# High and low parts of the left operands: two arrays each, or one array with the parts in turn

## The chip, the core and the metric

The kernel runs on one core of a Trainium2 chip. A time is the device time of one execution in microseconds (us). The profile is that of one execution; its span runs from the first to the last instruction that the profile holds. Less is better.

## The reference

One layer of a decoder, for 256 positions and a width of 2048, all in float32. Cut to what matters here:

```python
x = x + 0.5 * swiglu(rms_norm(x, ffn1_norm), ffn1_w_gate, ffn1_w_up, ffn1_w_down)   # width 5632
h = rms_norm(x, mix_norm)
proj = h @ w_in                                   # 10256 columns
aq, ak, av, bq, bk, bv, br, bz, ga, gb = split(proj)
o_a = dilated_attention(rope(rms_norm(aq)), rope(rms_norm(ak)), av)   # 8 heads of 128
log_a = log_sigmoid(bz @ b_gate_w2 + b_gate_bias) / 16                # rank 16
o_b = rms_norm(gated_linear_attention(bq, bk, bv, log_a)) * silu(br)  # 4 heads
y = sigmoid(ga) * (o_a @ w_a_up) + sigmoid(gb) * (o_b @ w_b_up)
x = x + y @ w_out
x = x + 0.5 * swiglu(rms_norm(x, ffn2_norm), ffn2_w_gate, ffn2_w_up, ffn2_w_down)
```

## The kernel before

**Products in three parts.** Nearly all the work is matrix products with large weights. TensorE multiplies operands of the type float32r, which keeps fewer bits than float32. So each operand is held as a high part (the value rounded to float32r) and a low part (the rest), and a product is the sum of three: high x high, high x low and low x high. `split` makes the parts: ScalarE copies the value into the high part, VectorE subtracts that from the value and writes the low part. `split_scaled` does the same with a factor.

**The two sides of a matmul.** The left operand (`lhsT`, the activations, transposed so that the contraction lies on the 128 partitions) is loaded into the array; it is the stationary side, 128 columns wide. The right operand (`rhs`, the weights of the layer, 512 columns) streams through it; it is the moving side. In this text a load is the loading of a stationary operand, which the profile shows as LDWEIGHTS on an engine of its own, PEld. Results are summed in PSUM in two tiles of 128 rows and 512 columns (`acc`, one for each half of the 256 positions, the index t).

**The loop.** All big products are cut into jobs (a block of 512 columns of a weight matrix) and those into steps of two slices of 128 of the contraction. Step i loads 512 KB of weights (`dma_to`), splits them (`split_to`, three steps ahead, into tiles `wh` and `wl`) and issues 12 matmuls (`multiply`, line 150): two slices, two halves of the positions, three products. There are 752 such steps. Other work, such as activations, transposes, the attention and the gated linear attention, is put between the steps by hand-written step numbers and by a list of tasks with costs.

**The left operands.** They are `xh` and `xl` (the normed x, transposed; 16 slices of 256 positions), `fhh` and `fhl` (the inner activations of the first FFN, 44 slices; `shh` and `shl` for the second), `ah` and `al` (outputs of attention, 8 slices) and `bh` and `bl` (outputs of the gated linear attention, 8 slices). In each array the positions of a slice lie next to each other, 4 bytes apart. A load takes 128 of them:

```python
a_hi, a_lo = job.lhs(k, t)
lhsT, rhs = ((a_hi, hi), (a_hi, lo), (a_lo, hi))[j]
nc.tensor.matmul(job.acc[t], lhsT, rhs[:, kk, :], ...)
```

`x_transposed`, `to_lhs`, `y_lhs`, `b_lhs`, the attention's `values` and, for the first norm, `split_xt` write these arrays. One product uses `xh` and `xl` as the moving side: `low_rank` (line 427), 32 matmuls with 32 stationary columns each, for the gate's code z.

**Other names in the rows.** `gram` (line 565), `o` (lines 581 to 583) and `s` (line 730) are plain float32 products of the two attentions, in which the profile shows two passes for each product. Line 550 multiplies `e_tiles` by q or k, in place, at eight levels: at level l it takes runs of 2^l elements and leaves as many out, so at level 0 every second element, on both inputs and the output.

Of the kernel before, what the change touches and what calls it, by code (L numbers as in the profile page):

```python
# [9 lines left out]
F32 = mybir.dt.float32  # L10
F32R = mybir.dt.float32r
# [7 lines left out]
P = 128  # L19
D_MODEL = 2048  # L20
SEQ = 256
D_FF = 5632
NT = SEQ // P
NC = 512
KM = D_MODEL // P
NM = D_MODEL // NC
NF = D_FF // NC
KF = D_FF // P
# [8 lines left out]
BH = 4  # L37
# [20 lines left out]
LINE = 128  # L58
# [11 lines left out]
def hybrid_block(ctx, tc, a):  # L70
    nc = tc.nc
    ctx.enter_context(tc.manual_schedule())
    const = ctx.enter_context(tc.tile_pool(name="const", bufs=1))
# [4 lines left out]
    def side(name):  # L78
        return pside.tile([P, NC], F32, tag="side", name=name)

    x = const.tile([P, NT, D_MODEL], F32, name="x")
    xh = const.tile([P, KM, SEQ], F32R, name="xh")
    xl = const.tile([P, KM, SEQ], F32R, name="xl")


    subs = []
# [6 lines left out]
    def at(step, fn, *args):  # L93
        events.setdefault(step, []).append((fn, args))
# [83 lines left out]
    def finish(flag):  # L178

        while not flag():  # L180
            ready = [t for t in tasks if is_ready(t)]
            assert ready
            run_stage(ready[0])

    def add_task(gen, *needs, delay=2):
        tasks.append({"gen": gen, "needs": needs, "next": now[0] + delay})
# [4 lines left out]
    def row(src, n):  # L191

        return bass.AP(tensor=src.tensor, offset=src.offset, ap=[[0, P], [1, n]])
# [57 lines left out]
    def split(hi, lo, src):  # L251
        nc.scalar.copy(hi, src)  # L252
        nc.vector.tensor_tensor(lo, src, hi.bitcast(F32), op=ALU.subtract)  # L253
# [23 lines left out]
    class FFN:  # L277
# [14 lines left out]
        def open(self):  # L292
            self.stack = ExitStack()
            self.pool = self.stack.enter_context(tc.tile_pool(name=f"{self.name}h", bufs=1))
            self.hh = self.pool.tile([P, KF, SEQ], F32R, name=f"{self.name}hh")
            self.hl = self.pool.tile([P, KF, SEQ], F32R, name=f"{self.name}hl")

        def lhs_h(self, k, t):
            return self.hh[:, k, t * P:(t + 1) * P], self.hl[:, k, t * P:(t + 1) * P]
# [58 lines left out]
    class Mixer:  # L358
# [36 lines left out]
        def open(self, i):  # L395
            self.stack = ExitStack()
            self.pool = self.stack.enter_context(tc.tile_pool(name="mix", bufs=1))
            self.stats = self.t([P, LINE], "stats")
            self.sum_mask = self.t([P, 12, P], "sums", dt=F32R)
            self.wz = self.t([P, KM, 4 * 2 * RANK], "ob", dt=F32R, name="wz_parts")[:, :, :2 * RANK]  # L400
            w = self.t([P, KM, RANK], "temp", 3, name="wz")
            nc.sync.dma_start(w, a["w_z"])
            at(i + 6, split, self.wz[:, :, :RANK], self.wz[:, :, RANK:], w)
            self.w2 = self.t([2 * RANK, NC], "pt", 2, name="w2")
            self.gate_bias = self.t([P, NC], "pt", 2, name="gate_bias")
            for j in range(2):
                nc.sync.dma_start(self.w2[j * RANK:(j + 1) * RANK], a["b_gate_w2"])
            nc.sync.dma_start(self.gate_bias, row(a["b_gate_bias"], NC))

            def load_mask(name, out):  # L410
                m = self.temp(f"c_{name}")
                nc.sync.dma_start(m, a[f"c_{name[:-1]}"][:, 4 * int(name[-1]):][:, :4, :].rearrange("p l t -> p (l t)"))
                out = out.rearrange("p l t -> p (l t)")
                at(now[0] + 3, nc.scalar.copy if out.dtype == F32R else nc.vector.tensor_copy, out, m)

            for j in range(3):
                at(i + 4 + j, load_mask, f"sums{j}", self.sum_mask[:, 4 * j:4 * j + 4, :])
            for j in range(2):
                at(i + 8 + j, load_mask, f"pick{j}", small["pick"][:, 4 * j:4 * j + 4, :])
            at(i + 9, self.low_rank)  # L420
# [32 lines left out]

        def decays(self):

            self.lag = [self.t([P, NT, NC], f"sA{j}", dt=F32R, name=f"lag{j}") for j in range(2)]
            for t in range(NT):
                p = side(f"gate{t}")
                nc.tensor.matmul(p, self.z[:, t * P:(t + 1) * P], self.w2, start=True, stop=True)
                g, e = self.temp(f"gate{t}"), self.temp(f"lse{t}")  # L460
                nc.vector.scalar_tensor_tensor(g, p, norm_mix.r[:, t:t + 1], self.gate_bias,
                                               op0=ALU.mult, op1=ALU.add)
                yield 0.6, 1
                nc.scalar.activation(e, g, AF.Abs)
                nc.scalar.activation(e, e, AF.Exp, scale=-1.0)
                nc.scalar.activation(e, e, AF.Ln, bias=1.0)
                yield 0.0, 1
                nc.vector.scalar_tensor_tensor(e, g, 0.0, e, op0=ALU.min, op1=ALU.subtract)
                yield 0.6, 1
                split(self.lag[0][:, t, :], self.lag[1][:, t, :], e)  # L470
                yield 0.6, 0
            self.flags.add("lag")

        def take_b(self, what, acc):
            r = self.rows(f"{what}_rows")
            for t in range(NT):
                self.scaled(r[:, t, :], acc, t)
            if what == "bk":
                self.bT = self.t([P, 2, BH, SEQ], "bh", name="bT")
            add_task(self.b_transposed(what, r))  # L480

        def b_transposed(self, what, r):
# [121 lines left out]
        def take_br(self, n, acc, t):  # L604
            finish(self.o_done)
            if n == 0 and t == 0:
                self.bh = self.t([P, 8, SEQ], "bh", dt=F32R)
                self.bl = self.t([P, 8, SEQ], "bl", dt=F32R)
            ns = slice(n * NC, (n + 1) * NC)
            e = self.temp(f"br{n}_{t}")  # L610
            nc.scalar.activation(e, acc[t], AF.Tanh, scale=norm_mix.half[:, t:t + 1])
            nc.vector.scalar_tensor_tensor(e, e, 1.0, acc[t], op0=ALU.add, op1=ALU.mult)
            o = self.ob[:, t, ns]
            nc.vector.scalar_tensor_tensor(o, e, norm_mix.half[:, t:t + 1], o,
                                           op0=ALU.mult, op1=ALU.mult)
            if t == NT - 1:
                add_task(self.b_lhs(n))
            return 1.2
# [89 lines left out]
        def attention(self, g):  # L708
            if g == 0:
                finish(self.flag("lag_used"))  # L710
                self.ah = self.t([P, 8, SEQ], "sA0", dt=F32R, name="ah")
                self.al = self.t([P, 8, SEQ], "sA1", dt=F32R, name="al")
            qT, kT, v, ast = self.aT[g][:, 0], self.aT[g][:, 1], self.av[g], self.ast_of[g]
            units = [(0, 0, 4), (1, 0, 2), (1, 2, 2)]
            pts = {}
# [320 lines left out]
```

## Time and profile before

| | us |
|---|---|
| median of 2 runs | 2146.95 (2145.76 to 2148.15) |
| profiled execution | 2146.12 |
| its span | 2144.3 |
| TensorE matmul busy | 2137.9 (100%) |
| TensorE loads busy | 1771.7 (83%) |
| VectorE busy | 1146.1 (53%) |
| ScalarE busy | 946.7 (44%) |

Matmuls are pipelined: a busy interval of TensorE is no proof that it works at its best pace, and the recorded durations of neighbours overlap. The distance from one start to the next is the pace. The ends of matmuls are modelled in the profile.

### The profile page before, as it was taken

How to read it: one execution, taken by the hardware profiler on the slowest of the kernel's cores; microseconds unless marked ns; L12 is line 12 of the kernel's file. 1: busy time of each engine (PE TensorE's matmuls, PEld its weight loads, DVE VectorE, ACT ScalarE, POOL GpSimd, SP SyncE). 2: the span in 40 equal slices, each digit the busy share in tenths (PEclk: the TensorE clock that was granted, in tenths of full speed). 3: DMA queues.
4: the chain of work that ended last, by engine and by line, in shares of the span. 5: the costliest groups of instructions: out<-in, count | busy, mean ns of one | idle time of the engine just before them, and what ended most of it. 6: DMA issues, size and time to landing. Idle time of an engine off the chain costs nothing.

```text
span 2144.3 us, 24974 instructions
## 1 busy us (share of the span) xinstructions
PE 2137.9 (100%) x9684; PEld 1771.7 (83%) x9684; DVE 1146.1 (53%) x1308; ACT 946.7 (44%) x1099; POOL 15.8 (1%) x15
## 2 busy tenths in 40 slices
PE   9999999999999999999999999999999999999999
PEld 7888888888888888888888888888888888888887
DVE  6655555554554456766644466565555555554443
ACT  6444444444444464454444444454444444443332
POOL 0000000000000000000000000000000000000000
PEclk9999999999999999999999999999999999999999
DMA  8666666665565664455566655656666666666663
GB/s 303 205 189 188 192 190 187 190 193 188 191 191 188 190 197 138 149 170 173 170 193 195 194 188 186 188 185 189 191 187 190 189 193 188 188 191 202 205 204 121
DMA packets 114519, 404.53 MB, mean 189 GB/s; under 512 B 13376, under 2 KB 14912, under 8 KB 114400
## 3 DMA queue, kind: packets, MB, share of 16 engines
q1 hardware_dynamic: 114400, 402.93, 60.2%
q8 instruction: 76, 1.25, 0.2%
q14 instruction: 43, 0.35, 0.0%
HBM read 400.79 MB, written 2.10 MB: 188 GB/s over the span
## 4 chain that ended last, share of the span: by engine, by line
PE 99%; DMA 0%; SPq 0%; ACT 0%; DVE 0%; issue 0%; DVEq 0%
PE acc_sg L150 11%; PE acc_fd L150 11%; PE acc_sd L150 11%; PE acc_su L150 11%; PE acc_fu L150 11%; PE acc_fg L150 11%; PE acc_o L150 4%; PE acc_ga L150 4%; PE acc_gb L150 4%; PE acc_aq L150 2%; PE acc_ak L150 2%; PE acc_bv L150 2%; PE acc_br L150 2%; PE acc_av L150 2%; PE acc_ua L150 2%; PE acc_ub L150 2%
## 5 line engine op out<-in xcount | busy, mean ns | idle before, releaser
L253 DVE TENSOR_TENSOR wl_sd<-w_sd,wh_sd 128x1024 fp32r<-128x1024 f32 x88 | 107.8, 1225 | 126.3 <-ACT wh_sd L252 126.3
L253 DVE TENSOR_TENSOR wl_fd<-w_fd,wh_fd 128x1024 fp32r<-128x1024 f32 x88 | 107.8, 1225 | 120.5 <-ACT wh_fd L252 120.2
L253 DVE TENSOR_TENSOR wl_su<-w_su,wh_su 128x1024 fp32r<-128x1024 f32 x88 | 107.8, 1225 | 118.4 <-ACT wh_su L252 118.4
L253 DVE TENSOR_TENSOR wl_fu<-w_fu,wh_fu 128x1024 fp32r<-128x1024 f32 x88 | 107.7, 1225 | 116.7 <-ACT wh_fu L252 113.2
L253 DVE TENSOR_TENSOR wl_sg<-w_sg,wh_sg 128x1024 fp32r<-128x1024 f32 x88 | 107.8, 1225 | 107.8 <-ACT wh_sg L252 107.8
L253 DVE TENSOR_TENSOR wl_fg<-w_fg,wh_fg 128x1024 fp32r<-128x1024 f32 (+1 forms) x90 | 108.1, 1201 | 97.7 <-ACT wh_fg L252 97.7
L252 ACT CAST wh_sd<-w_sd 128x1024 fp32r<-128x1024 f32 x88 | 92.8, 1055 | 146.5 <-PE acc_sd L150 139.8
L252 ACT CAST wh_sg<-w_sg 128x1024 fp32r<-128x1024 f32 x88 | 92.7, 1053 | 134.7 <-PE acc_su L150 66.6
L252 ACT CAST wh_su<-w_su 128x1024 fp32r<-128x1024 f32 x88 | 92.8, 1055 | 133.7 <-PE acc_sg L150 73.2
L252 ACT CAST wh_fg<-w_fg 128x1024 fp32r<-128x1024 f32 (+1 forms) x90 | 93.0, 1034 | 130.4 <-PE acc_fg L150 65.9
L252 ACT CAST wh_fd<-w_fd 128x1024 fp32r<-128x1024 f32 x88 | 92.7, 1053 | 129.5 <-PE acc_fd L150 119.7
L252 ACT CAST wh_fu<-w_fu 128x1024 fp32r<-128x1024 f32 x88 | 92.7, 1055 | 126.7 <-PE acc_fg L150 71.1
L150 PE MATMUL acc_fg<-wh_fg,xh 128*128 128x512 f32 x352 | 138.6, 395 | 0.7 <-DVE xh L873 0.7
L150 PE MATMUL acc_fg<-wl_fg,xh 128*128 128x512 f32 x352 | 137.7, 392 | 0.3 <-DVE wl_fg L253 0.3
L150 PE MATMUL acc_sg<-wh_sg,xh 128*128 128x512 f32 x352 | 137.9, 392 | 0.0
L150 PE MATMUL acc_fd<-wh_fd,fhh 128*128 128x512 f32 x352 | 137.3, 390 | 0.0
L150 PE MATMUL acc_fg<-wh_fg,xl 128*128 128x512 f32 x352 | 137.3, 391 | 0.0
L150 PE MATMUL acc_sg<-wh_sg,xl 128*128 128x512 f32 x352 | 137.1, 389 | 0.0
L150 PE MATMUL acc_sd<-wh_sd,shh 128*128 128x512 f32 x352 | 137.0, 389 | 0.0
L150 PE MATMUL acc_sg<-wl_sg,xh 128*128 128x512 f32 x352 | 137.0, 389 | 0.0
L150 PE MATMUL acc_fd<-wh_fd,fhl 128*128 128x512 f32 x352 | 137.0, 389 | 0.0
L150 PE MATMUL acc_fd<-wl_fd,fhh 128*128 128x512 f32 x352 | 137.0, 389 | 0.0
(306 smaller groups left out, 4985.0 us busy)
## 6 DMA issues: line engine op xcount, KB each, us to landing
w_fu<-in_ffn_w_up SPq DMA_DIRECT2D x88, 512.0 KB, 3.6
w_fd<-in_ffn_w_down SPq DMA_DIRECT2D x88, 512.0 KB, 3.5
w_sg<-in_ffn_w_gate SPq DMA_DIRECT2D x88, 512.0 KB, 3.6
w_su<-in_ffn_w_up SPq DMA_DIRECT2D x88, 512.0 KB, 3.6
w_sd<-in_ffn_w_down SPq DMA_DIRECT2D x88, 512.0 KB, 4.3
w_fg<-in_ffn_w_gate SPq DMA_DIRECT2D x86, 512.0 KB, 3.6
w_ga<-in_w_in SPq DMA_DIRECT2D x32, 512.0 KB, 3.6
w_gb<-in_w_in SPq DMA_DIRECT2D x32, 512.0 KB, 3.5
```

Source lines behind the costliest of these rows:

```text
L150: nc.tensor.matmul(job.acc[t], lhsT, rhs[:, kk, :], start=(k == 0 and j == 0), stop=(k == job.kt - 1 and j == 2))
L252: nc.scalar.copy(hi, src)
L253: nc.vector.tensor_tensor(lo, src, hi.bitcast(F32), op=ALU.subtract)
```

## The change

The two arrays of each left operand become one with a last axis of 2, in which element 0 is the high part and element 1 the low part of the same value. `parts_of` gives the two views, in which neighbours are 8 bytes apart. All functions that write or read left operands work on these views and are otherwise the same. The tile tags follow: `ah` and `al` share the place of `lag` (tag "ap"), `bh` and `bl` that of `bT` (tag "bp"). Two places move: a tile of 8 elements (`to_place`) lies ahead of the FFN's array, which so starts 32 bytes later, and `stats` is 16 elements longer, so that the tiles behind it in the mixer start 64 bytes later, or, behind the joined arrays, elsewhere.

In the built program every engine has the same instructions in the same order as before, with the same waits; tile names, steps and places are what differs.

```diff
     x = const.tile([P, NT, D_MODEL], F32, name="x")
-    xh = const.tile([P, KM, SEQ], F32R, name="xh")
-    xl = const.tile([P, KM, SEQ], F32R, name="xl")
+    def parts_of(t):
+
+        return t[:, :, :, 0], t[:, :, :, 1]
+
+    xh, xl = parts_of(const.tile([P, KM, SEQ, 2], F32R, name="xp"))
...
-            self.hh = self.pool.tile([P, KF, SEQ], F32R, name=f"{self.name}hh")
-            self.hl = self.pool.tile([P, KF, SEQ], F32R, name=f"{self.name}hl")
+            self.pool.tile([P, 8], F32, tag="to_place", name=f"{self.name}to_place")
+            self.hh, self.hl = parts_of(self.pool.tile([P, KF, SEQ, 2], F32R, name=f"{self.name}hp"))
...
-            self.stats = self.t([P, LINE], "stats")
+            self.stats = self.t([P, LINE + 16], "stats")
...
-            self.lag = [self.t([P, NT, NC], f"sA{j}", dt=F32R, name=f"lag{j}") for j in range(2)]
+            lag = self.t([P, 2, NT, NC], "ap", dt=F32R, name="lag")
+            self.lag = [lag[:, j] for j in range(2)]
...
-                self.bT = self.t([P, 2, BH, SEQ], "bh", name="bT")
+                self.bT = self.t([P, 2, BH, SEQ], "bp", name="bT")
...
-                self.bh = self.t([P, 8, SEQ], "bh", dt=F32R)
-                self.bl = self.t([P, 8, SEQ], "bl", dt=F32R)
+                self.bh, self.bl = parts_of(self.t([P, 8, SEQ, 2], "bp", dt=F32R))
...
-                self.ah = self.t([P, 8, SEQ], "sA0", dt=F32R, name="ah")
-                self.al = self.t([P, 8, SEQ], "sA1", dt=F32R, name="al")
+                self.ah, self.al = parts_of(self.t([P, 8, SEQ, 2], "ap", dt=F32R))
```

## Rows read from the trace of the kernel before

**Rows 1.** The page: busy times, granted clock in 40 slices, the chain by engine.

```profile
PE 2137.9 (100%) x9684; PEld 1771.7 (83%) x9684; DVE 1146.1 (53%) x1308; ACT 946.7 (44%) x1099; POOL 15.8 (1%) x15
...
PEclk9999999999999999999999999999999999999999
...
PE 99%; DMA 0%; SPq 0%; ACT 0%; DVE 0%; issue 0%; DVEq 0%
```

**Rows 2.** Waits of PE: us in total, times, longest.

```profile
PE warm L859 <- DVE warm L853: 1.2, 1, 1.2
PE acc_fg L150 <- DVE xh L873: 0.7, 1, 0.7
PE acc_fg L150 <- DVE wl_fg L253: 0.3, 1, 0.3
```

**Rows 3.** Windows, whole span, line 150 alone; the columns are named in the first row.

```profile
core 0: us, PE busy (x) PEld busy (x), PEclk, DMA share, GB/s
0.00:2145.00 2145.00, 2069.28 (x9024) 1690.78 (x9024) 1.00 0.60 189
```

**Rows 4.** Timeline of PE in the steady loop: start, duration, instruction.

```profile
1500.00 0.39 PE L150 MATMUL acc_sg<-wh_sg,xh 128*128 128x512 f32 x1
1500.22 0.39 PE L150 MATMUL acc_sg<-wl_sg,xh 128*128 128x512 f32 x1
...
1504.08 0.39 PE L150 MATMUL acc_sg<-wh_sg,xh 128*128 128x512 f32 x1
```

**Rows 5.** Line 427, the low-rank product: durations, then first and last start.

```profile
L427 PEld LDWEIGHTS z<-xh,wz_parts x16: 107/108/108, 761.6 to 765.3; 128*32 128x32 f32 x16
L427 PE MATMUL z<-xh,wz_parts x16: 280/280/281, 761.9 to 765.4; 128*32 128x256 f32 x16
```

**Rows 6.** Groups by form, a load and a matmul of line 150: busy us, mean ns.

```profile
L150 PEld LDWEIGHTS acc_sg<-wh_sg,xl 128*128 128x128 f32 x352 | 66.1, 188 | 13.8
L150 PE MATMUL acc_sg<-wl_sg,xh 128*128 128x512 f32 x352 | 137.0, 389 | 0.0
```

**Rows 7.** Groups of PEld from 822.59 to 823.9 us, the gram's loads.

```profile
L565 PEld LDWEIGHTS gram<-e_tiles 128*128 128x128 f32 x11 | 1.3, 192 | 0.0
```

**Rows 8.** Timeline of PEld behind the scores' loads.

```profile
1005.28 0.19 PEld L150 LDWEIGHTS acc_br<-wh_br,xh 128*128 128x128 f32 x1
1005.39 0.19 PEld L150 LDWEIGHTS acc_br<-wl_br,xh 128*128 128x128 f32 x1
```

**Rows 9.** Timeline of DVE, line 550: levels 0 to 3, then 4 to 7.

```profile
816.86 1.70 DVE L550 TENSOR_TENSOR e_tiles<-e_tiles,bT 128x128 f32<-128x128 f32 x8
...
819.61 1.70 DVE L550 TENSOR_TENSOR e_tiles<-e_tiles,bT 128x128 f32<-128x128 f32 x8
```

**Rows 10.** Groups of PE from 2140.25 us to the end: the last matmul.

```profile
L150 PE MATMUL acc_sd<-wh_sd,shl 128*128 128x512 f32 x1 | 0.4, 388 | 0.0
```

**Rows 11.** Timeline of PE behind transposes of the attention.

```profile
943.96 0.39 PE L150 MATMUL acc_aq<-wl_aq,xh 128*128 128x512 f32 x1
...
944.42 0.40 PE L150 MATMUL acc_aq<-wh_aq,xh 128*128 128x512 f32 x1
944.66 0.39 PE L150 MATMUL acc_aq<-wl_aq,xh 128*128 128x512 f32 x1
944.88 0.39 PE L150 MATMUL acc_aq<-wh_aq,xl 128*128 128x512 f32 x1
...
946.04 0.39 PE L150 MATMUL acc_aq<-wl_aq,xh 128*128 128x512 f32 x1
```

**Rows 12.** Groups by form, the writers of left operands.

```profile
L253 DVE TENSOR_TENSOR fhl<-fht,fhh 128x512 fp32r<-128x512 f32 x22 | 14.1, 682 | 0.0
...
L249 DVE SCALAR_TENSOR_TENSOR xl<-xt,g_f,xh 128x256 fp32r<-128x256 f32 x16 | 7.3, 480 | 4.3 <-ACT xh L248 4.3
...
L252 ACT CAST fhh<-fht 128x512 fp32r<-128x512 f32 x22 | 11.7, 586 | 0.0
...
L248 ACT ACTIVATE xh<-xt,g_f 128x256 fp32r<-128x256 f32 x16 | 7.1, 471 | 8.0 <-DVE xl L249 8.0
...
L873 DVE TENSOR_SCALAR xh<-x,g_f 128x256 fp32r<-128x256 f32 x4 | 1.4, 351 | 4.4 <-DMA g_f<-in_ffn_norm 3.8 <-DMA x<-in_xT 0.5
```

**Rows 13.** Timeline: the last part of x for the second FFN, and that FFN's first matmul.

```profile
1421.93 0.48 DVE L249 SCALAR_TENSOR_TENSOR xl<-xt,g_f,xh 128x256 fp32r<-128x256 f32 x1 [0.54 <-ACT xh L248]
...
1411.16 0.39 PE L150 MATMUL acc_sg<-wh_sg,xh 128*128 128x512 f32 x1
```

**Rows 14.** Timeline of PE, plain float32 products of the gated linear attention.

```profile
849.67 0.59 PE L581 MATMUL o<-bv_at 128*128 128x256 f32 x2
850.10 0.59 PE L582 MATMUL o<-bv_at 128*128 128x256 f32 x2
850.53 0.59 PE L583 MATMUL o<-bv_at 128*128 128x256 f32 x2
```

## The prediction

> **What bounds the kernel now.** I read the page first: its busy times, its clock line and the chain that ended last [rows 1]. TensorE is busy for 2137.9 us of 2144.3 us, the granted clock stands at 9 tenths or more in all 40 slices, and the chain is 99% TensorE. VectorE is busy for 53% and ScalarE for 44%. The waits of TensorE on others come to 2.2 us, all of them in the start [rows 2]. So the time is the pace of TensorE, and the next view has to say what that pace is made of.
>
> The loop's line L150 issues 9024 matmuls, each with one weight load [rows 3]. The durations in the table of groups (about 389 ns) overlap, so I take the pace from the starts: from 1500.00 to 1504.08 us there are 19 starts, 18 steps in 4.08 us, 226.7 ns each [rows 4]. [...] At one turn (0.417 ns) a column, 512 columns take 213.3 ns, and 13.3 ns of each step are something else. 9024 x 226.7 ns = 2045 us; the other 99 us of the span are small matmuls, transposes, start and tail. The profiled execution took 2146.12 us, 1.8 us more than its span; the median of the two runs shown is 2146.95 us, 0.8 us above it. I sum against 2146.1 and give the result on the median's scale. One nanosecond on the step of the loop is 9.0 us, and 2%, about what a measurement of this kernel can tell from no change, is 42.9 us or 4.8 ns a step.
>
> **The change, part by part.** No instruction is added, removed or moved: every engine's rows stand in the same order with the same waits as before, only under other tile names. So there is no new wait to price. What differs is the step between neighbouring elements (8 bytes in place of 4) of the arrays that hold left operands, and where some tiles lie. This touches four kinds of access.
>
> *1. The weight load.* All 9024 loads of L150 now take every second element of a row. A load of 128 columns is recorded with 188 ns [rows 6], one of 32 columns with 108 ns [rows 5], so a column costs (188 - 108) / 96 = 0.83 ns and 81 ns are a fixed part. How soon loads can follow each other is seen where the matmuls between them are short: eleven loads of the gram lie in 1.3 us, (1300 - 192) / 10 = 111 ns apart [rows 7], and two loads of L150 itself start at 1005.28 and 1005.39 us, 110 ns apart [rows 8]. In the steady loop a load starts as the matmul ahead of it starts, and has 226.7 ns. So 116 ns of each step are free on the load side. The trace shows no load with an 8-byte step. Its bounds: at the same 0.83 ns a column nothing changes; at twice that (one column in two turns) loads follow at 111 + 107 = 218 ns, still under 226.7, and nothing changes either; at three times it is 325 ns and the load becomes the bound (priced below). Nearest are rows of VectorE, the only engine whose accesses at an 8-byte step appear by themselves: L550 multiplies in place with input, second input and output all stepped, and its first eight instructions of a head (levels 0 to 3, where every second element, then runs of 2, 4 and 8 are taken) last 1.70 us, the next eight (levels 4 to 7, runs of 16 to 128) also 1.70 us [rows 9]. A step of 8 bytes there costs nothing that the row shows. I take 0 for the load.
>
> [...]
>
> *2. How a load and a running matmul meet.* The extra 13.3 ns might be the two streams of TensorE, moving and stationary, getting in each other's way; then the new step, which walks through memory twice as fast, could change it. Two rows speak of that. The last matmul of the program has no load behind it and is recorded with 388 ns [rows 10] against a mean of 389 ns with loads [rows 6]. And the 117 ns of the low-rank product, whose loads have only 32 columns, are 10 ns over the 106.7 ns of its columns: nearly the same surplus with a quarter of the load. Both say that the surplus belongs to the matmul itself and that the load costs it about 1 ns. Matmul ends are modelled in this profile, so the 388 alone would not carry it. Against it: just after other work the same matmuls need a dozen steps to settle. From 943.96 to 946.04 us nine steps take 2.08 us, 231 ns each, single steps between 0.22 and 0.24 us [rows 11], with the same instructions and operands as in the steady loop. So the relative timing of the streams can matter. Bounds by these rows: 0.22 us a step for ever would be 9024 x -6.7 ns = -60 us, 0.24 us would be +120 us, the settling mean of 231 ns +40 us. I take 0, by the rows of the lone matmul and of the short loads, and keep the ends for the range.
>
> [...]
>
> *3. The writers and VectorE's second input.* The high parts are written by ScalarE (L248, L252), the low parts by VectorE, which also reads the high part (L249, L253), all now at an 8-byte step. From the rows the low parts cost VectorE 14.1 + 14.1 + 7.3 + 7.3 + 5.3 + 5.1 us and three smaller groups, about 60 us, and the high parts ScalarE about 52 us [rows 12]. By L550 the cost is 0. If each doubled, VectorE would have 1206 us and ScalarE 999 us of work in 2144 us. What hides it there is the lead of the operands: the slices of x for the last norm are finished at 1422.41 us, while the matmuls that read this block first come 72 matmuls after acc_sg's first at 1411.16 us, at 1411.16 + 72 x 0.2267 = 1427.5 us [rows 13]. Its four pairs would end less than 4 us later if all doubled, inside those 5.1 us. Where that cover is missing, in the start, TensorE waits 0.7 us on L873 [rows 2], and four pairs of 351 and 478 ns there would add at most 4 x 0.83 = 3.3 us; I take 0.
>
> *4. The moving operand of the low-rank product.* Its 32 matmuls now stream the interleaved array: 0, or doubled 32 x 117 ns = 3.7 us. I take 0.
>
> Sum: 0 + 0 + 0 + 0, with at most 3.3 + 3.7 us from parts 3 and 4: 2147 us, for this case by itself 2129 to 2172 us: 2 ns of the step either way, twice the 1 ns that the lone matmul leaves for the load, and those 7 us upwards.
>
> **The rivals.**
>
> *The surplus goes (faster).* If the 13.3 ns are the price of loads and streams that cross, a load that moves at 8 bytes a column keeps another pace and may stay clear of the stream. The floor is the nearest stream with hardly any surplus, that of the fp32 products at 849.67, 850.10 and 850.53 us, pairs of passes of 256 columns: 215 ns a pass, with loads as large, and columns read at half the pace [rows 14]. 9024 x (215 - 226.7) = -105 us, 2041 us. It decides by 2% from a step of 221.9 ns down. For it: the settling steps, and that of the streams with large loads only the one read at full pace has the surplus. Against it: the lone matmul and the short loads.
>
> *Loads and streams meet more often (slower).* A load now reaches over 1020 bytes of a row in place of 512. If its meetings with the stream are the surplus and double with that, the step is 226.7 + 13.3 = 240 ns, +120 us, 2266 us; if the loop merely stays at the 231 ns of the settling stretch, +40 us, 2187 us. It decides from 231.4 ns up. For and against: the same rows, read the other way.
>
> *The load becomes the bound (slower).* From three turns a column, loads follow at 325 ns: 9024 x 98.3 ns = +887 us, 3034 us. It decides where 128 columns take more than 226.7 - 4 ns, 1.74 ns a column (111 - 107 = 4 ns being the part of a step that is no column). Against it: L550, where a stepped access is free.
>
> That the change would not do what it says is excluded: every left operand's slices have the step of 2.
>
> **How the numbers follow.** Same pace 0.62; surplus goes 0.17; loads meet more often 0.15; load as the bound 0.06. The forecast is the first, 2147 us. To leave out no more than 2 in 10, the range takes in the faster rival to its floor, 2040 us, and the milder half of the third case, up to 2190 us: 0.62 + 0.17 + about 0.07. Faster by over 2%: 0.17 x 0.94, about 0.16. Slower by over 2%: 0.15 + 0.06, about 0.20. Within 2%: the rest, 0.64.
>
> **What would show it.** Right: starts of L150 226.7 ns apart as before, loads of 188 ns, the groups of L248, L249, L252 and L253 with their old means, and 117 ns in the low-rank product. A load group at about 295 ns (81 + 2 x 107) with the same step would mean two turns a column, hidden. A step of 215 to 222 ns would show that the load had been the surplus after all, and part 2 wrong; 231 to 240 ns the same with the other sign. Load groups at 400 ns and TensorE gaps would show the load as the bound and part 1 wrong.

## The result, and the profile after

2204.07 us (2203.88 to 2204.26, two runs) against 2146.95 us: ratio 1.0266, 95% interval 1.0222 to 1.031, slower. The span of the profiled execution went from 2144.3 to 2202.5 us. In the changed file the matmul of the loop stands in line 153 (it was 150), the writers in 251, 252, 255 and 256 (248, 249, 252, 253), the low-rank product in 430 (427), the first norm's writer in 875 (873).

The page first: busy times, granted clock, chain by engine (as [rows 1]).

```profile
PE 2194.2 (100%) x9684; PEld 1825.7 (83%) x9684; DVE 1147.2 (52%) x1308; ACT 946.9 (43%) x1099; POOL 11.8 (1%) x15
...
PEclk9999999999999999999999999999999999999999
...
PE 99%; DMA 0%; SPq 0%; ACT 0%; DVE 0%; issue 0%; DVEq 0%
```

TensorE is still the whole chain, at the same clock, with the same counts; VectorE and ScalarE did not get more to do. The waits of PE (us in total, times, longest; as [rows 2]):

```profile
PE acc_fg L153 <- ACT wh_fg L255: 1.9, 1, 1.9
PE warm L861 <- DVE warm L855: 1.2, 1, 1.2
PE acc_fg L153 <- DVE wl_fg L256: 0.8, 1, 0.8
PE acc_fg L153 <- DVE xp L875: 0.3, 1, 0.3
```

They are 4.2 us in place of 2.2, all in the start. So the 58 us lie in TensorE's own pace, as the window of line 153 over the span says: 52.7 us more of matmul time than [rows 3], at granted clock 1.00 and with the same 9024 instructions.

```profile
0.00:2205.00 2205.00, 2121.93 (x9024) 1744.14 (x9024) 1.00 0.59 183
```

The timeline of PE gives that pace (start, duration, instruction; two rows of one name that follow each other stand as one, x2). The first and the last row of a stretch with 18 steps in the second FFN's up product, which reads x (`xp`); one with 18 steps in its down product, which reads the FFN's array (`shp`); and one with 15 steps in the output of the gated linear attention (`bp`):

```profile
1805.22 0.63 PE L153 MATMUL acc_su<-wh_su,xp 128*128 128x512 f32 x2
...
1809.42 0.63 PE L153 MATMUL acc_su<-wh_su,xp 128*128 128x512 f32 x2
...
2100.30 0.40 PE L153 MATMUL acc_sd<-wl_sd,shp 128*128 128x512 f32 x1
...
2104.48 0.39 PE L153 MATMUL acc_sd<-wl_sd,shp 128*128 128x512 f32 x1
...
1300.11 0.39 PE L153 MATMUL acc_ub<-wl_ub,bp 128*128 128x512 f32 x1
...
1303.56 0.39 PE L153 MATMUL acc_ub<-wl_ub,bp 128*128 128x512 f32 x1
```

4.20 us / 18 = 233.3 ns, 4.18 / 18 = 232.2 ns, 3.45 / 15 = 230.0 ns. Before, all three had 226.7 ns [rows 4]. There are 6528 matmuls that read x, 2112 on the FFN's arrays and 384 on the two attentions' outputs: 6528 x 6.67 + 2112 x 5.5 + 384 x 3.3 = 43.5 + 11.6 + 1.3 = 56.4 us. Three fixed values, one for each place to which the change moved an array, are the thing to see: a cost of the wider step alone would be one value.

The low-rank product, which streams `xp` as the moving side (first and last start; as [rows 5]):

```profile
L430 PEld LDWEIGHTS z<-xp,wz_parts x32: 107/128/131, 781.9 to 789.0; 128*32 128x32 f32 x32
L430 PE MATMUL z<-xp,wz_parts x32: 387/408/418, 782.1 to 789.3; 128*32 128x256 f32 x32
```

(789.3 - 782.1) / 31 = 232 ns in place of (765.4 - 761.9) us / 30 = 117 ns [rows 5]: 32 x 115 = 3.7 us. With the start's 2.0 us the parts come to 62 us against the 58.2 us of the span. Most of the difference is settling: before, matmuls behind other work had to come down to 226.7 ns from 231 ns or more [rows 11], and now they settle to a pace that is no better than that (230.0 to 233.3 ns). Beyond the paces above, the steps between neighbouring matmuls of the line took 11.6 us before and 10.5 us now, although the start's 2.0 us are in the second sum.

Loads and the last matmul (groups by form: busy us, mean ns; as [rows 6, 10]):

```profile
L153 PEld LDWEIGHTS acc_sg<-wl_sg,xp 128*128 128x128 f32 x352 | 68.0, 193 | 13.7
L153 PEld LDWEIGHTS acc_sd<-wl_sd,shp 128*128 128x128 f32 x352 | 68.8, 196 | 12.8
...
L153 PE MATMUL acc_sd<-wh_sd,shp 128*128 128x512 f32 x1 | 0.4, 397 | 0.0
```

The loads grew by 5 to 8 ns from 188 and are far from filling a step. The last matmul has no load behind it, and still grew from 388 to 397 ns; that will matter below. The writers (as [rows 12]):

```profile
L256 DVE TENSOR_TENSOR fhp<-fht,fhp 128x512 fp32r<-128x512 f32 x22 | 14.1, 683 | 0.0
L255 ACT CAST fhp<-fht 128x512 fp32r<-128x512 f32 x22 | 12.5, 619 | 0.0
L251 ACT ACTIVATE xp<-xt,g_f 128x256 fp32r<-128x256 f32 x16 | 7.4, 487 | 7.7 <-DVE xp L252 7.7
```

VectorE is where it was (682 before). ScalarE pays 33 ns for 512 columns and 16 ns for 256, in the shadow of the matmuls.

### The profile page after: what moved, and what is told of

Same layout as the page of the kernel before. It is cut to its first block, busy times and chain, and to the rows that moved or that the text cites. A ratio compares the mean times of both kernels' runs of the same rounds, so it can differ in the third digit from the quotient of the medians.

```text
span 2202.5 us, 24974 instructions
## 1 busy us (share of the span) xinstructions
PE 2194.2 (100%) x9684; PEld 1825.7 (83%) x9684; DVE 1147.2 (52%) x1308; ACT 946.9 (43%) x1099; POOL 11.8 (1%) x15
## 4 chain that ended last, share of the span: by engine, by line
PE 99%; DMA 0%; SPq 0%; ACT 0%; DVE 0%; issue 0%; DVEq 0%
PE acc_fu L153 11%; PE acc_su L153 11%; PE acc_sg L153 11%; PE acc_fd L153 11%; PE acc_sd L153 11%; PE acc_fg L153 11%; PE acc_gb L153 4%; PE acc_ga L153 4%; PE acc_o L153 4%; PE acc_ak L153 2%; PE acc_aq L153 2%; PE acc_bv L153 2%; PE acc_br L153 2%; PE acc_av L153 2%; PE acc_ua L153 2%; PE acc_ub L153 2%
## 5 line engine op out<-in xcount | busy, mean ns | idle before, releaser
L153 PE MATMUL acc_fg<-wh_fg,xp 128*128 128x512 f32 x704 | 225.5, 396 | 2.1 <-ACT wh_fg L255 1.9
L153 PE MATMUL acc_sg<-wh_sg,xp 128*128 128x512 f32 x704 | 225.2, 395 | 0.0
L153 PE MATMUL acc_fu<-wh_fu,xp 128*128 128x512 f32 x704 | 222.6, 394 | 0.0
L153 PE MATMUL acc_su<-wh_su,xp 128*128 128x512 f32 x704 | 222.6, 394 | 0.0
L153 PE MATMUL acc_fd<-wh_fd,fhp 128*128 128x512 f32 x704 | 221.6, 395 | 0.0
L153 PE MATMUL acc_sd<-wh_sd,shp 128*128 128x512 f32 x704 | 220.9, 394 | 0.0
L153 PEld LDWEIGHTS acc_fg<-wh_fg,xp 128*128 128x128 f32 x704 | 136.0, 193 | 31.2 <-ACT wh_fg L255 2.3
L153 PEld LDWEIGHTS acc_fu<-wh_fu,xp 128*128 128x128 f32 x704 | 135.9, 193 | 28.4
L153 PEld LDWEIGHTS acc_sd<-wh_sd,shp 128*128 128x128 f32 x704 | 137.6, 196 | 25.8
L153 PEld LDWEIGHTS acc_fd<-wh_fd,fhp 128*128 128x128 f32 x704 | 137.7, 196 | 25.6
```

The costliest lines, as they stand in the source:

```text
L153: nc.tensor.matmul(job.acc[t], lhsT, rhs[:, kk, :], start=(k == 0 and j == 0), stop=(k == job.kt - 1 and j == 2))
```

## The experiments

Theory A, after this reading: the pace belongs to float32r matmuls and their loads alone, and depends on where the stationary operand lies against the moving one as well as on the step. Theory B: the wider step costs by itself, wherever things lie, because a load covers twice the bytes. Theory C: something else of the change (writers, the joined arrays, memory traffic) slows TensorE down.

**Matmuls alone.** The layer is left out: two arrays are filled, then TensorE issues stretches of 96 matmuls, each with its load, from two slices of each operand in turn. The distance is that between the places of the stationary and the moving slice, modulo 256 bytes.

```python
        for j in range(COUNT):
            b = at + (j % 2) * 1024
            lhs = left[:, b:b + (cols - 1) * step + 1:step]
            m = (j % 2) * 1024
            rhs = flat_r[:, m:m + (n - 1) * mstep + 1:mstep]
            nc.tensor.matmul(acc[:cols, :n], lhs, rhs, start=j == 0, stop=j == COUNT - 1)
```

> This kernel leaves the whole layer out: it copies x to the output and runs 28 stretches of 96 float32r matmuls each, with no other engine at work, the stationary operand taken at steps of 1, 2, 3, 4 and 8 elements, at several places, with 32 to 128 columns, and the moving operand with 64, 256 or 512 columns, twice at a step of 2. If the step of the load is the cause by itself, the stretch with step one follows at 226.7 ns and the one with step two at about 233.3 ns, as in the layer's products from x. If the cause is the writers (ScalarE and VectorE at an 8-byte step, at work beside TensorE), both follow at the same pace, 226.7 ns or less. If only the place matters, step one and step two agree at the same place, and the stretches at 16, 32, 64 and 96 bytes differ from that at 0 for both steps. In the stretches of 64 moving columns the load sets the pace: 111 ns for step one if a column costs 0.83 ns, and 218 ns for step two if a stepped column costs two turns; the first theory needs more than 111 there, or else a meeting of load and stream that does not show when the load alone is the bound. The low-rank rows of the changed kernel predict 231 ns for the stretch of 256 moving columns at a step of 2.

The timeline of PE shows a stretch as one row (start, duration of the stretch):

```profile
39.15 22.56 PE L54 MATMUL steptwo<-right,left 128*128 128x512 f32 x96
...
130.26 22.47 PE L54 MATMUL oneatfour<-right,left 128*128 128x512 f32 x96
152.57 21.93 PE L54 MATMUL oneatsixteen<-right,left 128*128 128x512 f32 x96
174.34 22.55 PE L54 MATMUL oneathalf<-right,left 128*128 128x512 f32 x96
...
286.42 22.46 PE L54 MATMUL twoathalf<-right,left 128*128 128x512 f32 x96
308.71 22.25 PE L54 MATMUL twoatline<-right,left 128*128 128x512 f32 x96
...
353.19 22.39 PE L54 MATMUL onecolsthirtytwo<-right,left 128*32 128x512 f32 x96
...
514.29 11.68 PE L54 MATMUL twomid<-right,left 128*128 128x256 f32 x96
525.81 22.23 PE L54 MATMUL movetwo<-right,left 128*128 128x256 f32 x96
```

The pace is the duration, less the 0.39 us of the last matmul, over 95 steps; the values below are those of the settled part of a stretch. Step one: 226.7 ns at distance 0 and at 16 bytes, but 233.4 at 32 and at 64 and 232.4 at 4 bytes. Step two: 233.3 at 0, 232.3 at 32 bytes, 230.0 at 64 bytes. These last three are the paces of the changed kernel's three places: x at 0, the FFN's arrays 32 bytes and the attentions' 64 bytes off. No writer, no DMA and no other engine is at work here, so C falls; and contiguous loads at 32 bytes are as slow as the change, so B is not all of it. Other stretches: steps 3, 4 and 8 at distance 0 give 235.6, 235.1 and 245.3 ns; with 32 loaded columns and step one the pace is 231.6 ns, slower than the 226.7 with 128; with 256 moving columns it is 120.0 ns at either step, which with the 226.7 ns for 512 at distance 0 puts a column at (226.7 - 120.0) / 256 = 0.417 ns; with a moving operand at an 8-byte step and 256 columns it is 230.0 ns (`movetwo`), nearly twice that. The stretches with 64 moving columns ran at a granted clock of 0.57 and say nothing of loads; that was asked again below.

**The parts in turn by slices.** The change with its joined arrays, its names and its moved places, but with 256 high values and then 256 low values of a slice, each 4 bytes apart:

```diff
-        return t[:, :, :, 0], t[:, :, :, 1]
+        return t[:, :, 0, :], t[:, :, 1, :]
...
-    xh, xl = parts_of(const.tile([P, KM, SEQ, 2], F32R, name="xp"))
+    xh, xl = parts_of(const.tile([P, KM, 2, SEQ], F32R, name="xp"))
```

(and the same in the three other arrays)

> One array as in the change, at the same places, with the parts in turn slice by slice (256 high, then 256 low) instead of element by element, so every access is contiguous again. If the 8-byte step is the cause: 2147 us and steps of 226.7 ns. If the joining into one array or the moved places are the cause: 2204 us stays.

2163.61 us (2162.81 to 2164.79), ratio 1.0079 (1.0062 to 1.0096). Neither number came. The timeline of PE, 18 steps of the up product and 18 of the down product:

```profile
1804.76 0.39 PE L153 MATMUL acc_su<-wl_su,xp 128*128 128x512 f32 x1
...
1808.84 0.39 PE L153 MATMUL acc_su<-wl_su,xp 128*128 128x512 f32 x1
...
2099.77 0.40 PE L153 MATMUL acc_sd<-wl_sd,shp 128*128 128x512 f32 x1
...
2103.97 0.40 PE L153 MATMUL acc_sd<-wl_sd,shp 128*128 128x512 f32 x1
```

4.08 us (226.7 ns) where x is read, at distance 0; 4.20 us (233.3 ns) on the FFN's arrays, which lie 32 bytes off, and the same 64 bytes off. (2112 + 384) x 6.67 = 16.6 us, and 17.2 us were measured, against the 2146.38 us of the kernel before beside it. So joining the arrays costs nothing, and contiguous parts in a moved place are slow in the kernel too.

**The step without the moves.** The change without its two moved places, so that all arrays lie at distance 0:

```diff
-            self.pool.tile([P, 8], F32, tag="to_place", name=f"{self.name}to_place")
...
-            self.stats = self.t([P, LINE + 16], "stats")
+            self.stats = self.t([P, LINE], "stats")
```

> The change without its two shifts (no tile ahead of the FFN's array, statistics at their old length), so all left operands lie at multiples of 64 bytes. If the step alone sets the pace, all stages run at the 233.3 ns of the products from x: the down projections lose 1.1 ns on 2112 matmuls and the two up projections of the mixer 2.5 ns on 768, together +4 us, 2208 us. If the shifts are what costs the time, the time falls toward 2147 us.

```profile
2099.94 0.39 PE L153 MATMUL acc_sd<-wl_sd,shp 128*128 128x512 f32 x1
...
2104.14 0.39 PE L153 MATMUL acc_sd<-wl_sd,shp 128*128 128x512 f32 x1
```

2209.1 us (2207.2 to 2209.77), ratio 1.029 (1.0275 to 1.0306): 233.3 ns in all stages (4.20 us / 18 in the down product shown), 5 us over the change. So for contiguous parts the moves cost, and for parts in turn they help. (The two products on the attentions' outputs have 384 matmuls together; the expectation counted them twice.)

**Distances, one by one.** The stretches of the first experiment again, 64 matmuls each, behind a long warm stretch: step one at all distances from 0 to 124 bytes, step two at every second; the moving side moved in place of the stationary; both moved; plain float32 and bfloat16; and short bursts of 20 matmuls with 64 moving columns, 64 x 0.417 = 27 ns by the estimate above, against 111 ns from load to load [rows 7], so that the loads set their pace.

> Again the layer is left out: x is copied to the output, and TensorE runs stretches of 64 matmuls alone. Stretches: float32r with the stationary operand at every 4 bytes from 0 to 124 (step one) and every 8 bytes (step two); the moving operand moved by 16 to 112 bytes instead, and both moved by the same 32, 64 or 96 bytes; the stationary operand 128 to 512 bytes further; plain float32 with 256 columns and bf16 with 512 columns at steps one and two; and 20 matmuls of 64 columns with loads at steps 1, 2, 3, 4 and 8. If the pace is a lock between two reads of TensorE, it goes by the distance of the two operands' places modulo some power of two: moving both leaves 226.7 ns, moving the one or the other gives 227 to 235 ns in a pattern that repeats after 128 bytes or less, and 226.7 ns is a rare best. If the pace goes by the place of the stationary operand alone, moving both changes it as moving the one does, and moving the moving operand does nothing. If only a moving operand read at its full pace can be disturbed, plain float32 stays at 215 ns and bf16 at about 216 ns for both steps. Loads alone: 111 ns at step one; by the recorded durations of the loads before (188, 193, 253, 309, 331 ns) 116, 176, 232 and 254 ns at steps 2, 3, 4 and 8.

```profile
33.56 14.68 PE L61 MATMUL one_aa<-right,left 128*128 128x512 f32 x64
...
864.83 14.70 PE L61 MATMUL both_ca<-right,left 128*128 128x512 f32 x64
...
1163.16 2.31 PE L61 MATMUL loadone<-right,left 128*128 128x64 f32 x20
...
1174.49 2.43 PE L61 MATMUL loadtwo<-right,left 128*128 128x64 f32 x20
...
1199.84 4.65 PE L61 MATMUL loadfour<-right,left 128*128 128x64 f32 x20
```

Step one: 226.7 ns at distances 0 (`one_aa`, (14.68 - 0.39) / 63) and 120 only; the other 30 lie between 229.9 and 235.0, mean of all 32: 232.3. Step two: 229.9 to 233.4 at all 16, mean 231.9, never 226.7. Step one at 16 bytes has 233.3 here, where the first experiment had 226.7: the same distance, another pace. Moving both sides by 32, 64 or 96 bytes gives 226.7 (`both_ca`); moving the stationary by 256 or 512 gives 226.7, by 128 233.3 and by 384 232.3. So in these stretches 226.7 ns came with the distance modulo 256 bytes, not with either place. For other distances that is not shown: with the moving side moved by 16 to 112 bytes, three of seven paces agree with those of the stationary side at the same distance, and the others differ by 1 to 5 ns. Plain float32 passes of 256 columns and bfloat16 matmuls of 512 have 215.8 ns at steps 1 and 2 (at distance 0, the only one tried with them), where float32r has 226.7 and 233.3 ns. And the loads by themselves follow each other at 111.6 ns (step one) and 117.8 ns (step two), far below a step of the loop; at step four it is 233 ns, also in the first half of that burst, at granted clock 1.00.

**The other half, and other lengths.** Distances 128 to 252 bytes, loads of 32 columns, and other numbers of moving columns.

> The layer is left out again; TensorE alone, 64 float32r matmuls a stretch: the second half of the distances (128 to 252 bytes, step one every 4, step two every 8), loads of 32 columns at every 16 bytes from 0 to 240, and moving operands of 256 to 504 columns at distance 0 for both steps. If 226.7 ns at distance 0 is a lucky lock and not what step one costs, nearly all other distances stay between 229 and 236 ns for both steps, with means within 1 ns of each other (the first half gave 232.3 and 231.9), and loads of 32 columns, a quarter of the reads, run at the same 229 to 236 ns. If step one were cheaper by itself, its mean over places would be lower by several ns. If the surplus were paid for each read of the load, 32 columns would come to 217 ns. By the length of the stream: a surplus that belongs to the start of a matmul stays at 13 to 20 ns from 256 to 504 columns, one that is paid along the stream halves at 256.

```profile
77.27 15.09 PE L58 MATMUL one_ad<-right,left 128*128 128x512 f32 x64
92.19 14.68 PE L58 MATMUL one_ae<-right,left 128*128 128x512 f32 x64
...
1010.75 13.38 PE L58 MATMUL lend<-right,left 128*128 128x448 f32 x64
...
1094.81 13.18 PE L58 MATMUL twolend<-right,left 128*128 128x448 f32 x64
```

Step one: 226.7 at six more distances, 144 bytes (`one_ae`) among them, else 228.4 to 237.3; over all 64 distances the mean is 231.9 ns and 8 have 226.7. Step two: 229.9 to 233.4, mean 232.2. So at a place taken blindly the step costs 0.3 ns against contiguous loads, by the means; what it lacks is the good places. Loads of 32 columns: 228.2 to 240.0, mean 231.8, as for 128 columns. With seven lengths from 256 to 504 moving columns the surplus over the columns' own time (0.417 ns each) is 13 to 20 ns at either step, and at 448 step two is the faster one (203.4 against 206.7 ns, `twolend` and `lend`), at 480 the slower (220.0 against 216.7): it comes with each matmul and does not grow with its length (13.3 ns at 256 columns and at 512, step one).

**The kernel before, with the weights 32 bytes further.** Nothing of the change; the filler ahead of the weights' tiles grows by 8 elements, so that x lies 32 bytes off for its products and the other arrays stay at distance 0:

```diff
-    const.tile([P, 56], F32, name="to_line")
+    const.tile([P, 64], F32, name="to_line")
```

> The kernel before, with two separate arrays and contiguous parts, and one change: the padding ahead of the weight tiles is 32 bytes longer. All that lies behind it moves along, so the distance between left operand and weights changes by 32 bytes for the products from x alone (6528 of 9024 matmuls); the other products keep theirs. If the distance sets the pace: 6528 x 6.7 ns = +44 us, 2190 us, as slow as three quarters of the change without any change of step. If the 8-byte step is what costs: 2147 us.

2187.88 us (2186.81 to 2189.19), ratio 1.0191 (1.0174 to 1.0208). The products from x, 18 steps:

```profile
1805.00 0.39 PE L150 MATMUL acc_sg<-wh_sg,xl 128*128 128x512 f32 x1
...
1809.20 0.39 PE L150 MATMUL acc_sg<-wh_sg,xl 128*128 128x512 f32 x1
```

4.20 us, 233.3 ns; the down product stays at 226.7. So 32 bytes of filler take from the kernel before some 70% of what the change took. B as the whole cause falls.

**Parts in turn at their best place.** The change with all its arrays 64 bytes off, where step two had its least, 230.0 ns:

```diff
+    const.tile([P, 16], F32, name="to_place")
...
-            self.pool.tile([P, 8], F32, tag="to_place", name=f"{self.name}to_place")
+            self.pool.tile([P, 16], F32, tag="to_place", name=f"{self.name}to_place")
...
-    const.tile([P, 56], F32, name="to_line")
+    const.tile([P, 40], F32, name="to_line")
```

> The change, with all interleaved arrays put at the distance of 64 bytes from the weights at which the stretches of step two ran at 230.0 ns (the products from x and the FFNs' inner products were at 0 and 32 bytes, at 233.3 and 232.2 ns). If the distance sets the pace for the stepped load too: 9024 x (230.0 - 226.7) = +30 us and 3.6 us for the low-rank product, 2180 us. If the step alone sets it: 2204 us stays.

```profile
649.65 0.40 PE L154 MATMUL acc_fd<-wl_fd,fhp 128*128 128x512 f32 x1
...
653.85 0.40 PE L154 MATMUL acc_fd<-wl_fd,fhp 128*128 128x512 f32 x1
...
1804.83 0.39 PE L154 MATMUL acc_sg<-wl_sg,xp 128*128 128x512 f32 x1
...
1808.28 0.39 PE L154 MATMUL acc_sg<-wl_sg,xp 128*128 128x512 f32 x1
```

2182.02 us (2181.72 to 2183.1), ratio 1.0163 (1.0148 to 1.0179). Most of the loop runs at 230.0 ns (3.45 us / 15 in the second pair of rows), which alone makes 9024 x 3.33 + 3.7 = 33.8 us over before; 35 were measured. About a tenth of the loop's steps run at 233.3 ns (4.20 us / 18 in the first pair, in a stretch of 58 us), at the same distance and step. 22 us of the change's 57 were thus its places, and some 35 are what parts in turn keep here against the best place of contiguous parts.

**The kernel before at another good distance.** By the map, x at 144 bytes should have 226.7 ns as at 0:

```diff
-    xh = const.tile([P, KM, SEQ], F32R, name="xh")
-    xl = const.tile([P, KM, SEQ], F32R, name="xl")
+    const.tile([P, 32], F32, name="to_place")
+    xp = const.tile([P, 4 + 2 * KM * SEQ], F32R, name="xp")[:, 4:]
+    xp = xp.rearrange("p (j k s) -> p j k s", j=2, k=KM)
+    xh, xl = xp[:, 0], xp[:, 1]
...
-    const.tile([P, 56], F32, name="to_line")
+    const.tile([P, 16], F32, name="to_line")
```

> The kernel before, contiguous parts, with the two arrays of x moved by 144 bytes against the weights and everything else at its place. If the distance sets the pace by the map of the stretches (144 bytes ran at 226.7 ns, 128 at 232.1 and 160 at 233.3), the products from x keep 226.7 ns and the time stays at 2147 us, although the arrays no longer lie at a multiple of 32, 64 or 128 bytes. If what counts is that the left operands lie at such multiples (a line or a row of the memory), the 6528 matmuls from x lose 5 to 7 ns each, 2180 to 2192 us.

2186.9 us (2186.18 to 2187.95), ratio 1.0186 (1.0168 to 1.0205). A miss. Most of the products from x, here 15 steps of one, run at 233.3 ns (3.50 us / 15); parts of three others at 227.

```profile
1805.19 0.40 PE L152 MATMUL acc_sg<-wl_sg,xp 128*128 128x512 f32 x1
...
1808.69 0.39 PE L152 MATMUL acc_sg<-wl_sg,xp 128*128 128x512 f32 x1
```

So the distance alone does not fix the pace. What ran before might, which the last experiment asks.

**What runs before.** Matmuls alone again: each of five cases (step one at 0, 16 and 144 bytes, step two at 0 and 64) is entered from six different stretches: a, plain float32; b, 64 moving columns; c and d, distances 32 and 4; e, bfloat16; f, distance 0.

> The layer is left out; TensorE alone. Five cases (contiguous loads at distance 0, 16 and 144 bytes, step two at 0 and 64 bytes), 64 matmuls each, entered from six kinds of work before them: 8 plain float32 passes, 12 matmuls of 64 columns, 40 matmuls at distance 32, 40 at distance 4, 24 bf16 matmuls, 40 at distance 0. If the distance alone sets the pace, each case has one pace whatever came before it: 226.7 ns at 0 and one fixed value at 16 and at 144. If a distance allows several repeating patterns and the work ahead chooses, 16 and 144 bytes show both 226.7 ns and 231 to 235 ns, as 16 bytes did between the two earlier kernels (226.7 and 233.4) and 144 bytes between stretch (226.7) and layer (233.3), while distance 0 must end at 226.7 from every entry, as it does in the layer. Step two at 0 and 64 bytes: 233.3 and 230.0 ns from every entry if they are as single-valued as distance 0; a 226.7 among them would show that the step can be as fast.

```profile
35.96 14.77 PE L57 MATMUL onezero_a<-right,left 128*128 128x512 f32 x64
...
223.96 15.09 PE L57 MATMUL onesixteen_d<-right,left 128*128 128x512 f32 x64
...
284.31 15.17 PE L57 MATMUL onefar_a<-right,left 128*128 128x512 f32 x64
...
393.29 14.67 PE L57 MATMUL onefar_f<-right,left 128*128 128x512 f32 x64
...
518.46 15.10 PE L57 MATMUL twozero_f<-right,left 128*128 128x512 f32 x64
```

Step one at distance 0 comes to 226.7 ns from all six, within about seven steps. At 16 and at 144 bytes (`onefar`) it has 233.3 from five of them and 226.7 only where it takes over from distance 0 (`onefar_f`). Earlier stretches found the good pace there from elsewhere too: at 16 bytes from distance 4 (`oneatsixteen` behind `oneatfour`, where `onesixteen_d` of this experiment, also from distance 4, has 233.3), and at 144 bytes from 140 (`one_ae` behind `one_ad`). So the kind of work ahead does not settle it by itself; what more does is open. Step two has 233.3 at 0 and 230.0 at 64 bytes from all six, although in the layer parts ran at 233.3 at 64 bytes as well. That two paces hold at 144 bytes fits the map's point not carrying over: in the kernel other work comes between again and again. Distance 0 is the only good place that was tried from many entries and came to 226.7 ns from each, and the kernel before has all its arrays there.

## Why the prediction was wrong

**What bounds the kernel** was read rightly: TensorE's pace, 9 us for each nanosecond. No run shows how long a turn of the clock is. The 0.417 ns a column, and with it the 13.3 ns of a step that are not columns, is shown by matmuls alone: 120.0 ns for 256 columns and 226.7 ns for 512, at distance 0 and granted clock 1.00.

**Part 1, the load,** was right. Loads alone follow at 117.8 ns, within the bound of 111 to 218 ns; recorded durations rose by 5 to 8 ns, and the load stayed hidden. The rival that it becomes the bound had nothing behind it at this step.

**Part 2, how a load and a running matmul meet, is the step that failed.** "I take 0, by the rows of the lone matmul and of the short loads" rested on two rows that could not bear it. The last matmul's 388 ns were taken as a matmul undisturbed by a load. After the change the last matmul, again with none behind it, is recorded with 397 ns: the record grew by 9 ns with no load beside it. It does not follow the pace either: it is 397 ns also where the last stage ran at 230.0 ns (all arrays 64 bytes off) and at 233.3 ns (without the moves). So the 388 said nothing of what a load costs. The short loads of the low-rank product were taken to show that the surplus does not come from loads, since a quarter of the load left it as it was. Loads of 32 columns run at the same paces as loads of 128 (mean 231.8 against 231.9 ns over the distances), so the number of loaded columns could not tell the two apart. The row that pointed the right way was the settling at 231 ns [rows 11], the same instructions at another pace; the prediction named it as a bound and then gave it no weight in the sum. Measured, part 2 is 56 us, inside its own ends of -60 and +120 us.

An omission lies beside it: "where some tiles lie" is named among what differs and has no term in the sum. The two moved places alone add 17 us to contiguous parts, and take 5 us off the parts in turn.

For bfloat16 and plain float32 passes the pace was the same at both steps of the load (215.8 ns, at distance 0). For float32r it was not (226.7 and 233.3 ns there), and it went with the distance between the two operands, 226.7 to 237.3 ns over the map at step one.

**Part 3, the writers,** held: VectorE unchanged (682 to 683 ns for 512 columns), ScalarE 3 to 7% slower (471 to 487 and 591 to 630 ns), hidden. TensorE waits 0.3 us on line 875, under the 3.3 us allowed; the start's other waits rose by 2.4 us, which no experiment looked into.

**Part 4, the moving operand,** came out at its upper end: doubled, 3.7 us, where 0 was taken. Matmuls alone show it too, 230.0 against 120.0 ns.

**The rivals.** "Loads and streams meet more often" gave 231 to 240 ns and 2187 to 2266 us, and the result lies there. Its mechanism, that meetings double with the bytes a load covers, is not what was found: fewer loaded columns leave the mean over the distances as it was (at distance 0 they make it worse, 231.6 ns), and contiguous loads in an ordinary place are as slow (mean 231.9 against 232.2 ns). "The surplus goes" had a floor that float32r never reached: 226.7 ns is the least pace in all scans with 512 columns.

**What the cause is.** Shown: float32r matmuls with loads settle to a steady pace that goes by the distance between the operands and by the step (226.7 to 237.3 ns at step one, 229.9 to 233.4 at step two), and at some distances varies with what ran before (226.7 or 233.3 ns at 16 and at 144 bytes). The kernel before sits at distance 0, which came to the best pace from all six entries tried. With parts in turn, no distance tried reaches it: 229.9 ns is their least. The change thus gave up 30 us that only a good place had earned (best against best, 3.3 ns a step), 3.7 us in the low-rank product, and some 22 us more by where its arrays came to lie. Open: what the two reads share that makes these patterns (no stretch was run without loads, so that they meet is argued from the distance and not shown by itself), why 16, 64 and 144 bytes each show two paces, and why the paces are so often 226.67 or 233.33 ns. No version that was run beats the kernel before.

## What to carry to other kernels

Where the step of a matmul loop has one fixed value with a surplus over its columns, that value may be a pattern that the operands' places hold: before a layout is credited or blamed, move one side by 32 bytes and look at the starts again (226.7 and 233.3 ns here). Keep the moving side contiguous (120.0 against 230.0 ns for 256 columns here), and compare a layout with the best place of the old one, since a change of layout moves places too. The recorded duration of one pipelined matmul was no measure of the pace here (397 ns at 230.0 and at 233.3 ns); the distances from start to start are.

## What was not expected of the hardware

- The distance between stationary and moving operand changed the pace of float32r matmuls: 226.7 ns at 0 and 233.4 ns at 32 bytes, with the same instructions, 41 us in the kernel before.
- At 16 and 144 bytes two paces are stable, 226.7 and 233.3 ns, and which one a stretch takes varies with what ran before it.
- A moving operand of 256 float32r columns at an 8-byte step takes 228 to 232 ns in place of 117 to 120; a stationary one costs 6 ns in a load that is hidden.
- A load's pace by its step (1, 2, 4 and 8 elements): 111.6, 117.8, 233 and 238 ns for 128 columns. It doubles between steps two and four.
- ScalarE writes at an 8-byte step 3 to 7% slower (586 to 619 and 591 to 630 ns for 512 columns, 471 to 487 for 256); VectorE does not (682 to 683 ns).
